# Gate projections of a hybrid block by seven half-size products, with sums of weights made by accumulating transfers

## Chip, core and metric

One NeuronCore of a Trainium2 chip runs the whole program. The metric is device time in microseconds (us), lower is better. TensorE (PE) multiplies, VectorE (DVE) and ScalarE (ACT) do the elementwise work, GpSimd (POOL) and SyncE (SP) issue transfers here. Each engine takes its instructions strictly in the order of its own queue.

## What is computed

One layer of a model with 512 tokens of 1024 channels, preceded by 16 learned tokens. In short, with `*` elementwise:

```python
h  = concat(meta, x)                       # 528 x 1024
xn = rms_norm(h, norm_mix_g)
u_rnn, u_gate, q, k, v, g_ret, ga, gb = split(xn @ w_in)
o_a = rg_lru(causal_dwconv(u_rnn)) * gelu(u_gate)
o   = retention(rotary(q), rotary(k) / 16, v)        # 4 heads, 256 / 512 wide
o_b = head_rms(o) * silu(g_ret)                      # 2048 columns of w_in
mixed = sigmoid(ga) * (o_a @ w_branch_rnn) + sigmoid(gb) * (o_b @ w_branch_ret)
h = h + mixed @ w_out
gate, val = split(causal_dwconv(rms_norm(h) @ w_up))
out = rms_norm(h + (gelu(gate) * val) @ w_down)[16:]
```

All of it is float32 at the interface. The gate projections of the title are `g_ret`, `ga` and `gb`: 4096 columns of `w_in`.

## The kernel before

Every matrix is used as two float16 parts, a high and a low one (`split`, lines 86 to 88: ACT makes the high part, DVE the low part). A product is then three float16 products, high by high, high by low and low by high (`project`, line 264). Activations lie with channels on partitions, two halves of 257 tokens beside each other, so one projection of 128 columns over 1024 channels is 8 x 3 x 2 = 48 matmuls of 257 columns.

Weights come in units of 1 MB or less. `unit_load` has SP load a unit into one of two raw buffers (`raw`, pool `wraw`) and returns two steps, each of which splits half of it; the fp16 result lies in a `wt` tile. A raw buffer is loaded anew when its last split has read it. `get(u)` forces a unit's steps out, `tick()` emits one more step if it is not too far ahead of the products (`ahead`). A gate unit has 8 x 128 channels and 256 columns, that is two projections.

Up to the gate branch of the recurrence the order of PE, ACT and DVE is written by hand; from `order.close()` on, a scheduler orders the instructions of each engine by its own estimates when the program is built. That order then stands in the queues.

After the rotation come, for four heads, `scores(h)` (line 578), `values(h)` (line 623), `retention_out(h)` (line 645) and `gated(h)`. `retention_out` makes four blocks of 24 products; DVE (L649) and ACT (L651) empty each block's accumulation tile. `gated` projects `g_ret` for four blocks of 128 columns, normalizes the head (L660 to L664), multiplies (L676, L680) and splits the result. PSUM is cut into four accumulation tiles of two banks. The mix then runs eight rounds: two gate projections with a sigmoid each (L713), ten and sixteen channel blocks of the two branches (results taken at L719 and L726), their sum and its split.

SBUF has a pool `big` of 11 large slots, one for each whole tensor of a stage.

Of the kernel before, what the change touches and what calls it, by code (L numbers as in the profile page):

```python
# [50 lines left out]
def hybrid_block_kernel(ctx, tc, x, meta, norm_mix_g, w_in, conv_w, conv_b, rg_a_w, rg_a_b,  # L51
# [11 lines left out]
    def psum_layout(**pools):  # L63
        """Cuts the eight banks anew; each tile waits only for the users of its own banks."""
# [15 lines left out]
    def bigt(shape, dtype, name):  # L80
        return big.tile(shape, dtype, name=name, tag="big")
# [10 lines left out]
    def load(dst, src):  # L92
        """Large loads, kept in this order on their queue."""
        if last_load[0] is None:
            last_load[0] = nc.sync.dma_start(dst, src)
        else:
            with tc.issue_after(last_load[0].ins):
                last_load[0] = nc.sync.dma_start(dst, src)

# [6 lines left out]
    def unit(nk, ncol, parts):  # L106
        units.append((nk, ncol, parts))
        return len(units) - 1
# [18 lines left out]
    def add_gr(h):  # L127
        u_gr[h] = [unit(8, 256, [(0, 0, kmaj(w_in, 0, 8, o_gr + 512 * h + 256 * a, 256))]) for a in range(2)]
# [10 lines left out]
    for c in range(KD):  # L139
        u_g.append(unit(8, 256, [(0, 0, kmaj(w_in, 0, 8, o_ga + P * c, P)),  # L140
                                 (0, P, kmaj(w_in, 0, 8, o_gb + P * c, P))]))
# [8 lines left out]
    wviews = []  # L150

    def unit_load(pieces=2):
        """Loads the next unit; returns the steps that split it into fp16 parts."""
        nk, ncol, parts = units[len(wviews)]
        raw = wraw.tile([P, 2048], F32, name="raw")
        wt = wsp.tile([P, 2, 2048], F16, name="wt")
# [4 lines left out]
        wviews.append([wt[:, a, :n].rearrange("p (k c) -> p k c", k=nk) for a in range(2)])  # L161
        hf = n // pieces

        def step(a):
            sl = slice(a * hf, (a + 1) * hf)
            return lambda: split(wt[:, 0, sl], wt[:, 1, sl], raw[:, sl], SW)

        return [step(a) for a in range(pieces)]
# [3 lines left out]
    ahead = [4]  # L172
    current = [0]

    def advance(upto):
        """Emits the split steps (two for each unit) up to this count, loads one unit further."""
        while done[0] < min(upto, 2 * len(units)):
            while len(wviews) < min(done[0] // 2 + 2, len(units)):
                steps.extend(unit_load())
            steps[done[0]]()  # L180
            done[0] += 1

    def get(u):
        current[0] = max(current[0], u)
        advance(2 * u + 2)
        return wviews[u]

    def tick(n=1):
        """Splits n more half units if that is not too far ahead of the products."""
        advance(min(done[0] + n, 2 * current[0] + 2 + ahead[0]))  # L190

# [13 lines left out]
    xh = bigt([P, KD, T + 3], F16, "xh")  # L205
    xl = bigt([P, KD, T + 3], F16, "xl")
# [3 lines left out]
    gmix = bigt([P, D], F32, "gmix")  # L210
# [11 lines left out]
    def norm_rows(src, rows, g_bc, xn):  # L222
        rs = rms_scale(src, rows, "n")
        for a in range(2):
            sl = slice(a * 512, (a + 1) * 512)
            nc.vector.scalar_tensor_tensor(xn[:rows, sl], src[:, sl], rs[:rows], g_bc[:rows, sl],
                                           op0=ALU.mult, op1=ALU.mult)

    def norm_transpose(rows, xhd, xld, s, xn):
        for a in range(2):  # L230
            pv = bank("ptr").rearrange("p (b c) -> p b c", c=P)
            for k in range(4):
                c0 = (4 * a + k) * P
                nc.tensor.transpose(pv[:, k, :rows], xn[:rows, c0:c0 + P], ident[:rows, :rows])
            sl = slice(4 * a, 4 * a + 4)
            split(xhd[:, sl], xld[:, sl], pv[:, :, :rows], s)

    def norm_tile(src, rows, g_bc, xhd, xld, s, xn):
        norm_rows(src, rows, g_bc, xn)
        norm_transpose(rows, xhd, xld, s, xn)  # L240
# [3 lines left out]
    for i in range(2):  # L244
        xt = bigt([P, 2, D], F32, f"xin{i}")
        xin.append(xt)
    xmeta = bigt([P, D], F32, "xmeta")
# [723 lines left out]
```

## Time and profile before

| | us |
|---|---|
| median of three timed runs | 1116.58 |
| their lowest and highest | 1115.74, 1117.15 |
| span of the profiled execution (first to last instruction; the page lists no other time of it) | 1115.0 |

The page shows one profiled execution on the core. Its head gives each engine's busy time; "PEclk" is the clock that PE was granted, in tenths of full speed, in 40 slices of the span. A row of groups reads: line, engine, operation, written tile <- read tiles, shape, count | busy us, mean ns of one | idle time of the engine just before, and what ended it. In the table of stages a row reads: from:to, length, then busy time and count for each engine, PE's clock, the busy share of the 16 DMA engines and GB/s. A row of transfers reads: written <- read, issuing queue, count, KB each, median us from issue to landing.

### The profile page before, as it was taken

What the parts mean: (1) busy time and instruction counts of PE and PEld (TensorE: products, weight loads), DVE (VectorE), ACT (ScalarE), POOL (GpSimd) and SP (SyncE); (2) the same over time, 40 slices, a digit from 0 to 9 for tenths busy, and PEclk for the clock granted to TensorE, in tenths of its full rate; (3) what the DMA queues carried; (4) which work ended last, traced back from release to release, by engine and by line L of the source; (5) the groups of instructions that cost most, each with busy time, mean ns of one, the idle gap of its engine ahead of it and who ended that gap; (6) DMA issues with size and microseconds to landing.
All of it is one profiled execution on the core that took longest, in us unless ns stands there. A gap on an engine that the chain in (4) does not pass through costs nothing.

```text
span 1115.0 us, 19885 instructions
## 1 busy us (share of the span) xinstructions
PE 1100.0 (99%) x8931; PEld 844.4 (76%) x8931; DVE 604.7 (54%) x827; ACT 453.1 (41%) x626; POOL 5.5 (0%) x15
## 2 busy tenths in 40 slices
PE   7999999999999999999999999999999999999997
PEld 5888888865767588888888886588888888854443
DVE  6875799965565466433333332485666656542203
ACT  6558954423434354322222221364444434422202
POOL 1000000000000000000000000000000000000000
PEclk9999999999999999999999999999999999999999
DMA  6432333532222222333334352053233232332101
GB/s 201 138 114 76 103 106 114 181 125 76 76 76 77 76 62 62 100 100 100 100 100 138 114 178 88 1 190 114 81 110 102 89 114 80 111 114 92 60 1 76
DMA packets 111242, 111.95 MB, mean 100 GB/s; under 512 B 2228, under 2 KB 100114, under 8 KB 111156
## 3 DMA queue, kind: packets, MB, share of 16 engines
q1 hardware_dynamic: 110868, 110.53, 31.2%
q8 instruction: 70, 1.15, 0.4%
q0 software_dynamic: 288, 0.14, 0.1%
q14 instruction: 16, 0.13, 0.0%
HBM read 108.56 MB, written 2.10 MB: 99 GB/s over the span
## 4 chain that ended last, share of the span: by engine, by line
PE 87%; DVE 6%; ACT 5%; DMA 1%; issue 0%; SPq 0%; DVEq 0%; ACTq 0%
PE ps L264 57%; PE pd L882 11%; PE ps L623 8%; PE ps L797 3%; PE ps L645 3%; PE ps L279 2%; DVE wt L88 2%; PE ps L578 1%; DVE xr L442 1%; ACT wt L87 1%; DMA raw<-in_w_in 1%; ACT L495 1%; ACT r L433 1%; ACT t L429 1%; DVE t L441 1%; DMA xmeta<-in_meta_tokens 0%
## 5 line engine op out<-in xcount | busy, mean ns | idle before, releaser
L264 PEld LDWEIGHTS <-wt 128*128 128x128 f16 x6528 | 634.5, 97 | 97.0 <-DVE t L534 1.4
L264 PE MATMUL ps<-xh,wt 128*128 128x257 f16 (+2 forms) x2080 | 321.6, 274 | 1.7 <-DVE t L534 1.7
L88 DVE SCALAR_TENSOR_TENSOR wt<-raw,wt 128x1024 f16<-128x1024 f32 (+2 forms) x200 | 228.5, 1165 | 150.5 <-ACT wt L87 149.6
L87 ACT ACTIVATE wt<-raw 128x1024 f16<-128x1024 f32 (+2 forms) x200 | 192.7, 1004 | 200.0 <-PE ps L264 82.5
L264 PE MATMUL ps<-x2h,wt 128*128 128x258 f16 x1440 | 218.8, 273 | 0.0
L264 PE MATMUL ps<-xl,wt 128*128 128x257 f16 (+2 forms) x1040 | 200.5, 274 | 0.0
L264 PE MATMUL ps<-x2l,wt 128*128 128x258 f16 x720 | 137.7, 272 | 0.0
L882 PE MATMUL pd<-wt,act 128*128 128x512 f16 x576 | 124.7, 379 | 0.0
L849 DVE SCALAR_TENSOR_TENSOR cv<-ps,vt,cv 128x512 f32<-128x512 f32 x96 | 72.0, 751 | 85.8 <-ACT cv L847 84.1
L882 PEld LDWEIGHTS <-act 128*128 128x128 f16 x576 | 56.3, 98 | 68.0 <-issue 0.5
L264 PE MATMUL ps<-ob,wt 128*128 128x257 f16 x768 | 87.1, 274 | 0.0
L623 PE MATMUL ps<-wt,xh 128*128 128x512 f16 x256 | 76.2, 379 | 0.0
L847 ACT ACTIVATE cv<-ps,vt,vt 128x512 f32<-128x512 f32 x48 | 37.3, 777 | 76.5 <-PE ps L264 74.2
L264 PE MATMUL ps<-oah,wt 128*128 128x257 f16 x320 | 50.0, 274 | 0.0
L623 PE MATMUL ps<-wt,xl 128*128 128x512 f16 x128 | 48.3, 379 | 0.0
L623 PEld LDWEIGHTS <-xh 128*128 128x128 f16 x256 | 24.8, 98 | 29.2 <-issue 1.4
L797 PE MATMUL ps<-wt,mx 128*128 128x512 f16 x192 | 44.5, 378 | 0.0
L726 DVE SCALAR_TENSOR_TENSOR sg<-ps,sg 128x514 f32<-128x514 f32 x8 | 5.5, 694 | 57.9 <-PE ps L264 57.9
L88 DVE SCALAR_TENSOR_TENSOR v<-ps,v 128x512 f16<-128x512 f32 x20 | 13.8, 690 | 39.4 <-ACT v L87 39.4
L87 ACT ACTIVATE act<-cv 128x512 f16<-128x512 f32 x24 | 15.1, 630 | 45.2 <-DVE cv L868 45.2
L713 ACT ACTIVATE sg<-ps 128x514 f32<-128x514 f32 x16 | 9.6, 599 | 56.9 <-PE ps L264 56.9
L279 PEld LDWEIGHTS <-wt 128*128 128x128 f16 x288 | 27.8, 97 | 6.1 <-DVE wt L88 1.0
(176 smaller groups left out, 832.5 us busy)
## 6 DMA issues: line engine op xcount, KB each, us to landing
raw<-in_w_in SPq DMA_DIRECT2D x33, 1024.0 KB, 5.1
raw<-in_w_up SPq DMA_DIRECT2D x24, 1024.0 KB, 5.2
raw<-in_w_down SPq DMA_DIRECT2D x12, 1024.0 KB, 4.9
raw<-in_w_in SPq DMA_DIRECT2D x18, 512.0 KB, 5.2
raw<-in_w_branch_ret SPq DMA_DIRECT2D x8, 1024.0 KB, 5.7
raw<-in_w_branch_rnn SPq DMA_DIRECT2D x8, 640.0 KB, 4.4
raw<-in_w_out SPq DMA_DIRECT2D x4, 1024.0 KB, 4.9
xin<-in_x SPq DMA_DIRECT2D x4, 512.0 KB, 8.8
```

Of the source, the lines that this page charges most:

```text
L87: nc.scalar.activation(hi, src, AF.Copy, scale=s)
L88: nc.vector.scalar_tensor_tensor(lo, src, s, hi, op0=ALU.mult, op1=ALU.subtract)
L264: nc.tensor.matmul(ps[:, hf, :n], w_[:, k, col:col + P], x_[:, k0 + k, c0:c0 + n], start=start and k == 0 and a == 0, stop=stop and k == n ...
L279: nc.tensor.matmul(ps[:, hf, :n], w_[:, k, col:col + P], x_[:, k, c0:c0 + n], start=k == 0 and a == 0, stop=k == KD - 1 and a == 2)
L429: nc.scalar.activation(part(half_t, n), part(half_r, n), AF.Tanh, scale=cpos[:, n:n + 1])
L433: nc.scalar.activation(r, r, AF.Exp, scale=cneg[:, n:n + 1])
L623: nc.tensor.matmul(pb, x_[:, k, XF + j0:XF + j0 + nb], w_[:, k % 4], start=i == 0, stop=i == 23)
L645: nc.tensor.matmul(ps[:, hf, s0 - lo_i:257], vt[:, va, b, d * P:(d + 1) * P], st[:, sa, o:o + hi_i - s0], start=i == 0, stop=i == len(todo ...
L797: nc.tensor.matmul(ps[:, n], mk[:, a, c0:c0 + P], w_[:, k % 2, n * 512:(n + 1) * 512], start=j == 0, stop=j == 23)
L847: nc.scalar.activation(vv_, ps[:, :, 2:258], AF.Identity, scale=vt2[:, 96 + ch:97 + ch], bias=b_ff[:, ch:ch + 1])
L849: nc.vector.scalar_tensor_tensor(vv_, ps[:, :, j:j + 256], vt2[:, 48 * j + ch:48 * j + ch + 1], vv_, op0=ALU.mult, op1=ALU.add)
L882: nc.tensor.matmul(pd[tt][n], a[:, va, k % 5, tt * P:(tt + 1) * P], w_[:, k % 2, n * 512:(n + 1) * 512], start=k == 0 and va == 0 and w_ i ...
```

## The change

**Seven products for eight.** For a gate unit the 1024 channels are taken in two halves of four blocks, the 256 columns in two halves of 128, and the tokens in their two halves. So the unit is a 2 x 2 product of blocks, which the kernel before makes of eight half products of 12 matmuls, and the changed one of seven, by a Strassen-like scheme (`fast_products`). The products use B11, B21 and B22 of the weights and four sums T1 to T4, and A11, A12 and A22 of the input and four sums F3, F5, F6, F7 (`make_forms`, made once).

**Sums of weights.** Most are made by transfers: POOL issues a transfer from HBM that adds the block 11 onto the block 12 in the raw buffer (L215) as soon as the buffer is loaded; after the lower rows are cut into fp16 (`cut_low`), another adds the upper rows onto the lower ones (L204; in the mix two transfers of half the size). DVE then adds the right columns of the lower rows onto the left ones of both halves in place (`sums`, L212), and the raw buffer is cut again. A gate unit is split into 3.5 tiles of 1024 columns where it was two.

**Running sums.** Of the seven products four accumulate in one bank, `pa`, and two in another, `pe`; ACT copies the running sum out (`keep`, L723) before the next product goes on in `pa`. DVE adds the parts (L740, L744, L751). The last two products of a unit are left pending and come later.

**PSUM and SBUF.** During the heads and the mix PSUM has two accumulation tiles and four single banks. The pool `big` becomes 43 pieces of about 2 KB per partition and four large slots, `wsp` ten half-size tiles.

```diff
-    big = ctx.enter_context(tc.tile_pool(name="big", bufs=11))
+    xp = ctx.enter_context(tc.tile_pool(name="xp", bufs=4))
+    pieces = ctx.enter_context(tc.tile_pool(name="pieces", bufs=43))
     wraw = ctx.enter_context(tc.tile_pool(name="wraw", bufs=2))
-    wsp = ctx.enter_context(tc.tile_pool(name="wsp", bufs=5))
+    wsp = ctx.enter_context(tc.tile_pool(name="wsp", bufs=10))
...
+    def fast_steps(rv, parts):
+        tiles = []
+        top, low = slice(0, 4), slice(4, 8)
+        left, right = slice(0, P), slice(P, 2 * P)
+        def cut(rows, cols):
+            def run():
+                t = wsp.tile([P, 2, 1024], F16, name="wt")
+                src = rv[:, rows, cols]
...
+                split(tv[0], tv[1], src, SW)
+            return run
+        def add_low():
+            for _, c0, ap in parts:
+                nc.gpsimd.dma_start(rv[:, low, c0:c0 + ap.shape[2]], ap[:, 0:4], accum_op=ALU.add)
+        def cut_low():
+            cut(low, slice(0, 2 * P))()
+            add_low()
+        def sums():
+            both = rv.rearrange("p (i k) c -> p i k c", i=2)
+            nc.vector.tensor_tensor(both[:, :, :, left], both[:, :, :, left],
+                                    both[:, 1:2, :, right].broadcast_to([P, 2, 4, P]), op=ALU.add)
+        nc.gpsimd.dma_start(rv[:, top, right], parts[0][2][:, 0:4, 0:P], accum_op=ALU.add)
...
+        return [cut_low, cut(top, left), sums,
+                cut(top, slice(0, 2 * P)), cut(low, slice(0, 2 * P))]
...
+    def make_forms(g):
...
+        for i in range(2):
+            for j in range(2):
+                v = t[i, j] = wtile("xt")[:, :TQ].rearrange("p (k c) -> p k c", k=2)
...
+                nc.vector.tensor_tensor(v, xh[:, k0:k0 + 2, c0:c0 + n], xl[:, k0:k0 + 2, c0:c0 + n], op=ALU.add)
+        a11, a12, a21, a22 = t[0, 0], t[0, 1], t[1, 0], t[1, 1]
+        nc.vector.tensor_tensor(a22, a22, a21, op=ALU.subtract)
+        nc.vector.tensor_tensor(a21, a11, a21, op=ALU.subtract)
+        nc.vector.tensor_tensor(a12, a11, a12, op=ALU.subtract)
+        nc.vector.tensor_tensor(a12, a12, a22, op=ALU.add)
+        nc.vector.scalar_tensor_tensor(a11, a22, -1.0, a11, op0=ALU.mult, op1=ALU.subtract)
+        for i, v in enumerate((a12, a22, a11, a21)):
+            xs = x_form_t[i // 2]
+            split(xs[:, 2 * (i % 2), ks], xs[:, 2 * (i % 2) + 1, ks], v, 1.0)
...
+    def fast_products(w, src, func, scale, finish):
...
+        def keep(dst, ps):
+            nc.scalar.activation(dst, ps[:, :257], AF.Copy)
...
+        pa = bank("pa")
+        product(pa, "B11", "A11", True)
+        keep(kept[:, h0], pa)
+        yield
+        pe = bank("pe")
+        product(pe, "T3", "F7", True)
+        yield
+        product(pa, "T2", "F6")
+        keep(kept[:, h1], pa)
+        yield
+        pb = bank("pb")
+        product(pb, "B21", "A12", True)
+        nc.vector.tensor_tensor(g0[:, h0], pb[:, :257], kept[:, h0], op=ALU.add)
+        yield
+        product(pa, "T1", "F5")
+        keep(last[:, h0], pa)
+        nc.vector.tensor_tensor(g1[:, h1], pe[:, :257], last[:, h0], op=ALU.add)
+        yield
+        product(pa, "B22", "F3")
+        nc.scalar.activation(g1[:, h0], pa[:, :257], func, scale=-scale)
+        nc.scalar.activation(g1[:, h1], g1[:, h1], func, scale=-scale)
+        finish(1, g1)
+        product(pe, "T4", "A22")
+        nc.vector.tensor_tensor(g0[:, h1], pe[:, :257], kept[:, h1], op=ALU.add)
+        nc.scalar.activation(g0[:, :TQ], g0[:, :TQ], func, scale=scale)
+        finish(0, g0)
...
     scores(0)
     values(0)
+    make_forms(0)
     scores(1)
     scores(2)
+    make_forms(1)
     values(1)
     scores(3)
+    psum_layout(acc=2, bank=4)
+    ahead[0] = 9
     retention_out(0)
...
     for c in range(KD):
...
+        run = fast_products(get(u_g[c]), x_forms, AF.Sigmoid, 1.0 / (SW * S_XN),
+                            lambda j, g: sg.update({j: g[:, :TQ].rearrange("p (a b) -> p a b", a=2)}))
+        next(run)
+        flush()
+        for _ in range(4):
+            next(run)
             tick()
+        pa = acc("pa")
+        project(pa, get(u_ba[c]), 0, oa_of, HH, NR)
+        for _ in run:
+            pass
```

Two places show how the queues change. Names carry buffer numbers; `raw` is a weight buffer, `wt` an fp16 weight tile, `ps` an accumulation tile. First, DVE around the first two blocks of `retention_out(2)`, before:

```order
L88 SCALAR_TENSOR_TENSOR v3_4140<-ps_4261,v3_4140 128x512
L88 SCALAR_TENSOR_TENSOR wt_4459<-raw_4458,wt_4459 128x1024 x2
L88 SCALAR_TENSOR_TENSOR v3_4140<-ps_4201,v3_4140 128x512
L88 SCALAR_TENSOR_TENSOR wt_4576<-raw_4575,wt_4576 128x1024
L649 TENSOR_SCALAR or2_4280<-ps_4282 128x514
L88 SCALAR_TENSOR_TENSOR wt_4576<-raw_4575,wt_4576 128x1024
L649 TENSOR_SCALAR or2_4280<-ps_4309 128x514
```

And DVE at the same place in the changed kernel:

```order
L92 SCALAR_TENSOR_TENSOR wt_4798<-raw_4670,wt_4798 128x1024
L92 SCALAR_TENSOR_TENSOR v3_4457<-ps_4428,v3_4457 128x512
L92 SCALAR_TENSOR_TENSOR v3_4488<-ps_4487,v3_4488 128x512
L92 SCALAR_TENSOR_TENSOR wt_4815<-raw_4670,wt_4815 128x512
L805 TENSOR_SCALAR or2_4507<-ps_4512 128x514
L212 TENSOR_TENSOR raw_4670<-raw_4670 128x8x128
L805 TENSOR_SCALAR or2_4508<-ps_4539 128x514
L92 SCALAR_TENSOR_TENSOR wt_4847<-raw_4670,wt_4847 128x1024
```

The first row is the low cut of the unit gr3a, after which POOL issues the transfer; the sums that need it (L212) now stand between the emptying of the block's first and second accumulation tile. Second, ACT where a round of the mix begins, before (two splits of 640 of a branch unit, the split of the round's result, two gate functions, splits again):

```order
L87 ACTIVATE wt_5457<-raw_5456 128x640 x2
L87 ACTIVATE mx0_4995<-sg_5046 128x514
L713 ACTIVATE sg_5333<-ps_5284 128x514
L713 ACTIVATE sg_5390<-ps_5341 128x514
L87 ACTIVATE wt_5565<-raw_5564 128x1024 x2
```

And the same place in the changed kernel:

```order
L91 ACTIVATE wt_5750<-raw_5634 128x1024
L91 ACTIVATE wt_5755<-raw_5634 128x512
L723 ACTIVATE kept_5568<-pa_5572 128x257
L91 ACTIVATE mx_5558<-g0_5237 128x514
L91 ACTIVATE wt_5861<-raw_5634 128x1024
L723 ACTIVATE kept_5568<-pa_5572 128x257
L723 ACTIVATE last_5569<-pa_5572 128x257
```

The split `wt_5861` reads the raw buffer after its sums, and the copy of the running sum of `pa` stands behind it; PE's product T1 goes on in `pa` after that copy.

More of the change, by code (lines that the diff above doesn't have):

```diff
@@ L160, in unit_load @@
             load(rv[:, k0:k0 + ap.shape[1], c0:c0 + ap.shape[2]], ap)
[L161 to L168, printed above, removed]
+        loaded.append(len(loaded))
+        if fast:
+            return fast_steps(rv, parts)
+        hk = nk // 2
```

444 lines of the change are left out of this document (250 added, 194 removed).

## Prediction

> **What bounds the kernel now.** I read the page's head first, then what TensorE (PE) waits for, then the chain that ended last, then busy time by stage.
>
> ```profile
> span 1115.0 us, 19885 instructions
> PE 1100.0 (99%) x8931; PEld 844.4 (76%) x8931; DVE 604.7 (54%) x827; ACT 453.1 (41%) x626; POOL 5.5 (0%) x15
> PEclk9999999999999999999999999999999999999999
> ```
>
> The reader sees one engine that is always busy, at its full clock. A busy PE need not be a PE that never waits, so the next view is its waits, in full (us in total, times, longest):
>
> ```profile
> PE ptr L234 <- DVE xn L226: 2.1, 2, 1.6
> PE ps L264 <- DVE t L534: 1.7, 2, 1.1
> PE ps L313 <- DVE warm L308: 1.4, 1, 1.4
> PE ptr L234 <- DVE xl L88: 1.3, 2, 1.1
> PE ps L279 <- DVE wt L88: 0.7, 1, 0.7
> PE ptr L234 <- DVE xo L226: 0.5, 1, 0.5
> PE ps L279 <- DVE xl L88: 0.4, 1, 0.4
> ```
>
> They add up to 8.1 us, and none is at a gate (L264 waits only for the rotation, L534). The chain that ended last gives the pitch of the products (start, us, what):
>
> ```profile
> 290.04 7.43 PE ps L645 x96
> ...
> 319.69 15.60 PE ps L623 x72
> ...
> 436.66 240.69 PE ps L264 x2160
> ```
>
> 240.69 us / 2160 = 111.4 ns for a product of 257 columns. So this kernel is as long as its list of products, and whatever takes products out shortens it by 111.4 ns each, as long as nobody makes PE wait. VectorE (DVE) and ScalarE (ACT) have room on average; the stages touched need their own rows:
>
> ```profile
> core 0: us, PE busy (x) PEld busy (x) DVE busy (x) ACT busy (x) POOL busy (x), PEclk, DMA share, GB/s
> 231.40:290.00 58.60, 58.58 (x370) 30.64 (x368) 34.20 (x72) 23.61 (x42) 0.00 (x0) 1.00 0.18 59
> 290.00:342.00 52.00, 52.00 (x412) 36.12 (x409) 28.44 (x42) 21.12 (x30) 0.00 (x0) 1.00 0.23 77
> 342.00:393.70 51.70, 51.70 (x408) 35.81 (x406) 28.13 (x34) 21.02 (x28) 0.00 (x0) 1.00 0.27 82
> 393.70:430.40 36.70, 36.70 (x387) 32.62 (x384) 25.70 (x33) 17.79 (x25) 0.00 (x0) 1.00 0.31 82
> 430.40:452.70 22.30, 22.30 (x200) 19.44 (x197) 13.71 (x16) 9.34 (x13) 0.00 (x0) 1.00 0.18 54
> 452.70:677.35 224.65, 224.65 (x2017) 196.43 (x2016) 71.47 (x79) 58.88 (x74) 0.00 (x0) 1.00 0.40 118
> ```
>
> 231 to 290 is scores and values, 290 to 452.7 the four heads' retention and gates, 452.7 to 677 the eight rounds of the mix. In the heads DVE works 28.44+28.13+25.70+13.71 = 96.0 us of 162.7, in the mix only 71 of 225.
>
> **What the change takes out.** 16 gate units lose one of eight half products each, 12 matmuls of 257 columns: 192 in all, and the two instruction lists differ by just that number of 128x257 products. 192 x 111.4 ns = **21.4 us**, half in the heads (10.7), half in the mix (10.7).
>
> **What it adds on DVE and ACT.** Prices of one, and their spacing when they follow one another:
>
> ```profile
> L88 DVE SCALAR_TENSOR_TENSOR wt<-raw,wt 128x1024 f16<-128x1024 f32 x176 | 210.4, 1218 | 149.8 <-ACT wt L87 149.6
> L87 ACT ACTIVATE wt<-raw 128x1024 f16<-128x1024 f32 x176 | 177.2, 1046 | 147.7 <-issue 46.5 <-PE pd L882 39.0 <-PE ps L264 30.1
> L649 DVE TENSOR_SCALAR or<-ps 128x514 f32<-128x514 f32 x16 | 10.9, 686 | 0.3
> L713 ACT ACTIVATE sg<-ps 128x514 f32<-128x514 f32 x16 | 9.6, 599 | 56.9 <-PE ps L264 56.9
> ```
>
> ```profile
> 446.09 1.22 DVE L88 SCALAR_TENSOR_TENSOR wt<-raw,wt 128x1024 f16<-128x1024 f32 x1
> 447.23 0.69 DVE L88 SCALAR_TENSOR_TENSOR ob<-g,ob 128x514 f16<-128x514 f32 x1
> 447.83 1.22 DVE L88 SCALAR_TENSOR_TENSOR wt<-raw,wt 128x1024 f16<-128x1024 f32 x1
> ```
>
> A 1024-column operation holds DVE for 447.23-446.09 = 1.14 us, a 514-column one for 0.60; by that slope one of 257 takes 0.33 (estimate). Each gate unit gains 1.5 tiles of splitting (1.14+0.60), the in-place sums of 1024 elements (1.14, priced as a split) and three additions of 257 (0.99): **3.9 us of DVE**, 31 in the heads, 31 in the mix. ACT gains 1.5 splits and three copies of 257 columns (0.38 each, from 599 ns for 514 and 1046 for 1024): 2.7 us. The input's seven forms add 26 DVE operations of 514 columns, 15.6 us, in the stage that had 34.2 of 58.6 busy: 49.8, still under PE's time; I put 1 us on it (0 to 4).
>
> **What it adds in waits.** For each gate unit, DVE cuts the lower weight rows, GpSimd (POOL) issues the accumulating transfer onto them, and the sums (L212) stand in DVE's in-order queue until it lands. Let L be the time from the cut's end to the landing of 512 KB. No accumulating transfer is in this trace; the nearest rows:
>
> ```profile
> raw<-in_w_in SPq DMA_DIRECT2D x33, 1024.0 KB, 5.1
> ...
> raw<-in_w_branch_ret SPq DMA_DIRECT2D x8, 1024.0 KB, 5.7
> ...
> out<-h SPq DMA_DIRECT2D x2, 256.0 KB, 2.0
> xmeta<-in_meta_tokens SPq DMA_DIRECT2D x1, 64.0 KB, 5.5
> v<-in_ffn_conv_w POOLq DMA_DIRECT2D x1, 64.0 KB, 6.8
> ...
> v<-in_norm_ffn_g POOLq DMA_DIRECT2D x1, 4.0 KB, 5.3
> ```
>
> Between 256 and 1024 KB a plain transfer grows by 3.1 us, so 512 KB would take 3.0: the lower end. The upper end is POOL's 6.8 for 64 KB plus twice 2.0 for moving 512 KB (it must also read what it adds to): 10.8. POOL's rows fall in the start's crowd, where even 64 KB on SP took 5.5 against 2.0 for 256 KB at the end, so I take **L = 6.0** (5.3 + 2.0, less a part of the crowd). The Trainium skill, DMA: Bandwidth & Descriptors, section "Anatomy of one DMA", fits a transfer issued from GpSimd with 2.0 us plus its bytes at 436 GB/s; by that 512 KB takes 3.2 us (estimate), and the holes below would all but vanish; the POOL rows of this trace, 5.3 and 6.8 for 4 and 64 KB, do not agree with it.
>
> *Heads.* Work that DVE has between a unit's low cut and its sums, by the order of the changed kernel at the spacings above: 2.8, 2.8, 0.6, 1.8, 2.4, 2.2, 3.6 us for the seven units whose sums fall here (gr1, gr2, gr3 and the first mix unit). With L = 6 the holes are 3.2+3.2+5.4+4.2+3.6+3.8+2.4 = 25.8 us. DVE then has 96.0+31.0+25.8 = 152.8 us to spend while PE has 162.7-10.7 = 152.0: level, before any wait of DVE for PE. A second row says where it hurts: evacuations of PSUM stand behind the sums, and the heads now have two accumulation tiles where there were four. One block of retention is 24 products, 7.43/4 = 1.86 us; emptying it takes 0.69 (DVE) and 0.60 (ACT), so a tile comes back in time only if DVE comes at once. Walking heads 2 and 3 with these numbers: the tile of the values before retention 2 comes back 1.1 us late (hole of gr2b); block 2's last tile waits 3.0 us because its predecessor's evacuation follows L212 of gr3a; block 3's last tile waits 3.8 us behind L212 of gr3b. Heads 0 and 1 have values (15.60/3 = 5.2 us for a bank) to hide in: 1 us. Together **9 us**, and some 5 us more for each microsecond more of L, since five of these holes pass on in full.
>
> *Copies of a running sum.* Three products of each unit go on accumulating in a bank that ACT must copy out first. The cover is 12 products, 12 x 111.4 = 1.34 us; needed are the end of the last product, the copy of 0.38 and two semaphores:
>
> ```profile
> L264 PE MATMUL ps<-xh,wt 128*128 128x257 f16 x1600 | 246.0, 273 | 1.1 <-DVE t L534 1.1
> ```
>
> A product ends 273-111 = 0.16 us after the next may start; with 0.1 assumed for two semaphores the need is 0.64. In each head B22 of the first unit follows its T1 after only 4 products (0.45 us): 0.3 late; and once per head a split, a table load or a gate function stands ahead of the copy: some 0.5. **3 us** for four heads.
>
> *Mix.* Per round PE now has 84+60+96 = 240 products, 26.7 us. From the start of T1 (time 0): the copy, the second split of the summed rows and its low part end at 4.2; the buffer is free, the next 1024-KB branch load (5.7) lands at 10; B22 and T4 end at 10.9; DVE and ACT do the branch cuts, the evacuation and the low cut until 15.9; the round's last product ends at 21.4, its evacuation and the next additions at 23.5. The sums may start there, the copy after them ends at 26.3, T1 is due at 26.7. So the two transfers of 256 KB have 23.5-15.9 = 7.6 us, and the second issue costs about 0.6:
>
> ```profile
> 1.44 0.68 POOL L348 DMA_DIRECT2D v<-in_rnn_conv_w  x1
> ...
> 5.20 0.51 POOL L356 DMA_DIRECT2D v<-in_ffn_conv_w  x1
> ```
>
> At L = 6 that is 6.6, in time: **0**, and 1:1 in seven rounds beyond L = 7.0.
>
> *At nothing:* SBUF in pieces adds seven transfers on SP and no compute that I could not count above; SP's cover is its own idle time:
>
> ```profile
> SPq L98 <- DVE wt L88: 936.9, 96, 42.7
> ```
>
> 12 MB more from HBM go beside a DMA share of 0.18 to 0.40. Without that cover the branch load of the mix walk would land later, at the same 1:1.
>
> **The sum.** -21.4 + 9 + 3 + 1 + 0 = **-8.4 us**: the profiled span of 1115.0 becomes 1106.6. The timed runs have a median of 1116.58, 1.6 above that span, so the time is **1108** us. Anything under 0.2% (2.2 us) is no change that a measurement of this kernel tells.
>
> **Rivals.**
> 1. *The transfers are prompt* (L of 3 to 4). For: 3.0 us by the plain rows, and the skill's fit, named above, is of this kind. Against: POOL's rows. The 9 us go, 1 to 4 remain: -17.4 to -20.4, some 1098. Chance 0.20.
> 2. *The transfers are slow, and the kernel gets slower.* The place is L212 in DVE's queue, in the heads and at each round's start. At L = 8.5 the heads cost 9+12.5 and the mix 7 x 1.5 = 10.5: -8.4+23 = +14.6, 1131. It decides from L = 7.3, where -8.4 + 6.5 + 2.1 is about nothing. For: 6.8 for a mere 64 KB, and an addition reads twice. Against: the start's crowd in that row. Chance 0.25.
> 3. *The copies cost more than the transfers.* If a split of 1.0 us has always just begun when a copy is due, the need is 1.64 against 1.34: 0.3 us at two places in 16 units, 9.6 in place of 3: -1.8, 1115, no change. Against: in the mix ACT is mostly idle at these places. Chance 0.10.
>
> That it doesn't do what it says can be left out, since the 192 products are gone from PE's list and PE is the bound.
>
> **How the numbers follow.** The forecast (1102 to 1114) has 0.45. Faster is forecast and rival 1, less the edge of the forecast's band: 0.64; no change rival 3 and that edge: 0.11; slower 0.25. The range goes from rival 1 at 1098 to L = 8.5, 1130.
>
> **What would show it.** Right: L264 and the new product line together have 192 products fewer, at 111 ns; DVE's idle time before L212 is put to a DMA, some 26 us in the heads; PE's waits appear at L801 and at the values, on DVE or ACT, 2 to 4 us each from retention 2 on, and hardly any in rounds 1 to 7. The POOL rows give L itself. Wrong: no PE waits at L801 (L was short), or a wait at T1 in every round of the mix (L over 7), or waits of the product line on ACT copies all through.

## The result, and the profile after

| | us |
|---|---|
| after, median of four runs | 1162.42 (1161.54 to 1165.17) |
| before, four runs on the same chip | 1116.16 (1115.35 to 1117.15) |
| ratio, with its 95% interval | 1.042 (1.0405 to 1.0435) |
| span of the profiled execution after, before | 1163.4, 1115.0 |

The change makes the kernel 4.2% slower; 1108 was forecast, with 1130 as the upper end. The profiled execution of the changed kernel is the slowest of its four (1165.17 us), so differences of stages below add up to a little more than the difference of the medians. One execution of e9, further below, fell into a second, slower state of the chip (1233.11 us, granted clock 0.855) and is left out of its time. First the head of the changed kernel's page, as it was read for before.

```profile
span 1163.4 us, 19961 instructions
...
PE 1098.4 (94%) x8739; PEld 832.7 (72%) x8739; DVE 689.3 (59%) x951; ACT 501.9 (43%) x730; POOL 57.2 (5%) x55
...
PEclk9899999989999998998999999999999999999999
```

PE has 192 instructions fewer (8931 before), so the change does what it says. But its busy time is the same as before, 1098.4 against 1100.0, and it now idles 65 us of the span where it idled 15. Work was removed and no busy time went: the clock row tells most of the reason. It shows slices at 8 where before had only 9s, so the products that are left ran slower there. The table of stages of the changed kernel (up to the scores, scores and values, heads, mix, rest; its columns as before) places both:

```profile
0.00:237.70 237.70, 223.48 (x1913) 186.86 (x1914) 188.42 (x282) 144.95 (x204) 6.95 (x16) 0.99 0.39 128
237.70:303.90 66.20, 61.67 (x371) 31.40 (x370) 50.32 (x100) 26.67 (x49) 3.86 (x3) 0.95 0.26 64
303.90:476.40 172.50, 154.19 (x1230) 111.71 (x1227) 116.17 (x152) 80.33 (x129) 19.27 (x15) 0.95 0.44 100
476.40:725.80 249.40, 228.58 (x1995) 196.61 (x1993) 117.09 (x146) 93.02 (x138) 27.16 (x21) 0.97 0.56 138
725.80:1163.00 437.20, 430.47 (x3242) 306.09 (x3241) 217.31 (x274) 156.97 (x213) 0.00 (x0) 1.00 0.26 88
```

And the same stages, cut at the same instructions, of the kernel before:

```profile
0.00:231.30 231.30, 223.65 (x1914) 187.35 (x1915) 186.63 (x279) 144.47 (x201) 5.47 (x15) 0.99 0.42 135
231.30:289.90 58.60, 58.58 (x371) 30.64 (x369) 34.10 (x72) 23.55 (x42) 0.00 (x0) 1.00 0.18 58
289.90:463.20 173.30, 173.30 (x1496) 133.26 (x1492) 98.86 (x126) 73.56 (x102) 0.00 (x0) 1.00 0.27 80
463.20:677.20 214.00, 214.00 (x1923) 187.17 (x1921) 68.68 (x75) 54.64 (x68) 0.00 (x0) 1.00 0.40 118
```

The start is 6.4 us longer, the scores 7.6, heads and mix together 421.9 - 387.3 = 34.6, the rest is the same (437.2 and 437.8): 48.6 in the first four. (A few products cross the border between heads and mix, so these two are taken together.) In heads and mix PE idles 18.3 + 20.8 = 39.1 us, where it idled 0. Its busy time there is 382.8; before's 387.3 less 192 x 111.4 ns is 365.9. Most of the 16.9 us between are products at a lower clock. The granted clock allows at most 0.05 x 172.5 + 0.03 x 249.4 = 16.1, and part of that fell into time in which PE stood anyway; e1 below, at full clock, still has 3.1 us of such busy time, which leaves 13.8 for the clock (an estimate). So 39.1 + 16.9 - 21.4 = 34.6: **the products are gone, and waits and longer busy time take two and a half times what they saved.** What PE waits for, in the changed kernel:

```profile
PE pa L718 <- ACT kept L723: 22.1, 10, 7.6
PE ps L801 <- ACT sq L807: 7.2, 2, 4.4
PE ps L778 <- DVE v L92: 6.2, 3, 4.7
...
PE ps L778 <- DVE sf L656: 4.2, 1, 4.2
```

The first row is, nearly all of it, T1 waiting for the copy of the running sum. Its name misleads: the copy takes 0.38 us, and it is late because it stands behind the split of the sums. The other rows are evacuations (`sq`, `v`, `sf`) that stand in a queue behind the sums, or behind the work that the sums held up. The transfers and the wait for them, from three views of the changed kernel (who DVE waits for; median us from issue to landing; POOL's groups):

```profile
DVE raw L212 <- DMA raw<-in_w_in: 59.9, 15, 8.0
```

```profile
raw<-in_w_in POOLq DMA_DIRECT2D x32, 256.0 KB, 4.9
...
raw<-in_w_in POOLq DMA_DIRECT2D x8, 512.0 KB, 6.0
```

```profile
L204 POOL DMA_DIRECT2D raw<-in_w_in x24 | 31.5, 1488 | 123.7 <-DVE wt L92 98.7 <-ACT g L748 25.0
L215 POOL DMA_DIRECT2D raw<-in_w_in x16 | 20.6, 1289 | 486.0 <-DVE t L606 222.1 <-DMA raw<-in_w_in 171.3 <-ACT sq L807 38.8
```

From its issue a transfer of 512 KB lands after 6.0 us, as forecast. But one issue holds POOL for about 1.28 us (L215; L204's mean mixes single issues and pairs), not 0.6, and POOL's queue is in order. A round of the mix, from one T1 (556.09) to the next, in the changed kernel (start, us, engine; idle time before and its end in brackets):

```profile
560.97 0.74 ACT L91 ACTIVATE wt<-raw 128x640 f16<-128x640 f32 x1 [1.71 <-PE pa L339]
564.32 0.74 ACT L91 ACTIVATE wt<-raw 128x640 f16<-128x640 f32 x1 [2.62 <-PE pa L339]
...
572.34 1.06 ACT L91 ACTIVATE wt<-raw 128x1024 f16<-128x1024 f32 x1 [3.10 <-PE pb L339]
573.43 1.23 DVE L92 SCALAR_TENSOR_TENSOR wt<-raw,wt 128x1024 f16<-128x1024 f32 x1 [3.12 <-ACT wt L91]
574.95 2.59 POOL L204 DMA_DIRECT2D raw<-in_w_in  x2 [1.93 <-DVE wt L92]
...
583.13 1.23 DVE L212 TENSOR_TENSOR raw<-raw 128x1024 f32<-128x1024 f32 x1 [3.47 <-DMA raw<-in_w_in]
...
585.35 0.37 ACT L723 ACTIVATE kept<-pa 128x257 f32<-128x257 f32 x1
```

The round takes 585.77 - 556.09 = 29.7 us; 26.7 was forecast. The low cut ends at 574.66, 18.6 us after T1, where I had 15.9: the splits of the branch unit and the cut itself wait for PE to finish with a weight tile (the brackets of the first three rows). Then the pair of transfers is issued in 2.59 us and has landed 8.5 us after the cut (583.13 - 574.66), where I had 6.6. That is the longest of the seven rounds, which have 7.2 to 8.5. The sums come too late by 3 us, and PE waits 2.80 for `kept`.

### The profile page after: what moved, and what is told of

The parts are those of the page before. It is cut to its first block, busy times and chain, and to the rows that moved or that the text cites. A ratio compares the mean times of both kernels' runs of the same rounds, so it can differ in the third digit from the quotient of the medians.

```text
span 1163.4 us, 19961 instructions
## 1 busy us (share of the span) xinstructions
PE 1098.4 (94%) x8739; PEld 832.7 (72%) x8739; DVE 689.3 (59%) x951; ACT 501.9 (43%) x730; POOL 57.2 (5%) x55
## 3 DMA queue, kind: packets, MB, share of 16 engines
q0 software_dynamic: 21408, 12.73, 8.4%
## 4 chain that ended last, share of the span: by engine, by line
PE 62%; DVE 16%; DMA 11%; ACT 8%; issue 2%; POOL 1%; SPq 0%; DVEq 0%; ACTq 0%; POOLq 0%
PE ps L339 27%; PE pd L1051 11%; DMA raw<-in_w_in 10%; DVE wt L92 6%; PE ps L778 5%; PE pa L339 4%; PE pa L718 4%; ACT wt L91 3%; PE ps L968 3%; PE pb L339 3%; PE ps L352 2%; PE pe L718 1%; DVE raw L212 1%; DMA raw<-in_w_up 1%; DVE t L607 1%
## 5 line engine op out<-in xcount | busy, mean ns | idle before, releaser
L339 PEld LDWEIGHTS <-wt 128*128 128x128 f16 x4992 | 487.2, 98 | 84.1 <-ACT wt L91 5.8
L92 DVE SCALAR_TENSOR_TENSOR wt<-raw,wt 128x1024 f16<-128x1024 f32 (+2 forms) x232 | 262.1, 1139 | 181.6 <-ACT wt L91 180.8
L91 ACT ACTIVATE wt<-raw 128x1024 f16<-128x1024 f32 (+2 forms) x232 | 225.1, 984 | 257.4 <-PE pd L1051 54.0
L339 PE MATMUL ps<-xh,wt 128*128 128x257 f16 (+2 forms) x1056 | 165.1, 276 | 7.7 <-ACT wt L91 5.5
L718 PEld LDWEIGHTS <-wt 128*128 128x128 f16 x1344 | 132.5, 99 | 47.7 <-issue 26.5
L1020 DVE SCALAR_TENSOR_TENSOR cv<-ps,vt,cv 128x512 f32<-128x512 f32 x96 | 72.1, 751 | 58.5 <-ACT cv L1018 56.8
L339 PE MATMUL ps<-xl,wt 128*128 128x257 f16 (+2 forms) x528 | 103.0, 277 | 0.0
L718 PE MATMUL pa<-xs,wt 128*128 128x257 f16 x576 | 76.2, 283 | 22.9 <-ACT kept L723 22.1
L339 PE MATMUL pb<-ob,wt 128*128 128x257 f16 x768 | 87.1, 274 | 0.0
L339 PE MATMUL pa<-oa,wt 128*128 128x257 f16 x480 | 57.2, 280 | 0.0
L212 DVE TENSOR_TENSOR raw<-raw 128x1024 f32<-128x1024 f32 x16 | 19.6, 1226 | 59.9 <-DMA raw<-in_w_in 59.9
L215 POOL DMA_DIRECT2D raw<-in_w_in x16 | 20.6, 1289 | 486.0 <-DVE t L606 222.1
L801 PE MATMUL ps<-sc,v 128*128 128x257 f16 (+4 forms) x384 | 34.3, 248 | 9.0 <-ACT sq L807 7.2
```

Source lines behind the costliest of these rows:

```text
L91: nc.scalar.activation(hi, src, AF.Copy, scale=s)
L92: nc.vector.scalar_tensor_tensor(lo, src, s, hi, op0=ALU.mult, op1=ALU.subtract)
L212: nc.vector.tensor_tensor(both[:, :, :, left], both[:, :, :, left], both[:, 1:2, :, right].broadcast_to([P, 2, 4, P]), op=ALU.add)
L339: nc.tensor.matmul(ps[:, hf, :n], w(aw, k, col, P), src(ax, k, c0, n), start=k == 0 and (aw, ax) == (0, 0), stop=k == nk - 1 and aw == 1)
L718: nc.tensor.matmul(ps[:, :257], w(wf, aw, k), src(xf_, ax, k), start=first and k == 0 and (aw, ax) == (0, 0), stop=k == 3 and aw == 1, ski ...
L801: nc.tensor.matmul(ps[:, hf, s0 - lo_i:257], vt[b][:, va, d * P:(d + 1) * P], st[SCP[b][0]][:, sa, o:o + hi_i - s0], start=i == 0, stop=i ...
```

## The experiments

Each is an edit of the changed kernel. A time without an interval is one run.

**e1, without the accumulating transfers:**

```diff
-            for _, c0, ap in parts:
-                nc.gpsimd.dma_start(rv[:, low, c0:c0 + ap.shape[2]], ap[:, 0:4], accum_op=ALU.add)
+            pass
...
-        nc.gpsimd.dma_start(rv[:, top, right], parts[0][2][:, 0:4, 0:P], accum_op=ALU.add)
```

> The changed kernel without its accumulating transfers (the sums of weights lack what they add; the seven products and everything else stay). Theory T, the waits for the transfers: DVE's 59.9 us at L212 and the PE waits in heads and mix that follow from them vanish, with the half clock behind them; PE waits in heads and mix fall from 39 us to under 10, time 1106 to 1122 us. Rival S, the structure (two accumulation tiles, copies of the running sum, slots of weight tiles): waits move to those, time stays over 1145.

Measured: **1110.46 us**, 52 below the changed kernel. Heads and mix, in its table of stages:

```profile
297.10:463.00 165.90, 161.67 (x1363) 120.73 (x1361) 127.54 (x170) 90.99 (x148) 0.00 (x0) 1.00 0.24 77
463.00:671.10 208.10, 207.31 (x1863) 181.06 (x1862) 105.36 (x128) 83.18 (x120) 0.00 (x0) 1.00 0.43 134
```

374.0 in place of before's 387.3, 13.3 saved of 21.4, at full clock. So copies, additional splits, additions and single banks together cost 8.1 us there (5.0 in which PE idles, 3.1 of busy time above 365.9), and the transfers all the rest.

**e2, the same sums made by DVE**, in place of the transfers:

```diff
-                nc.gpsimd.dma_start(rv[:, low, c0:c0 + ap.shape[2]], ap[:, 0:4], accum_op=ALU.add)
+            nc.vector.tensor_tensor(rv[:, low], rv[:, low], rv[:, top], op=ALU.add)
+            nc.vector.tensor_tensor(rv[:, top, right], rv[:, top, right], rv[:, top, left], op=ALU.add)
...
-        nc.gpsimd.dma_start(rv[:, top, right], parts[0][2][:, 0:4, 0:P], accum_op=ALU.add)
```

In the program the two additions stand right ahead of L212's, no longer right behind the low cut.

> The sums that transfers made are made by DVE in the raw buffer: one addition of 1024 and one of 512 columns more for a gate unit, 1.1 + 0.6 = 1.7 us, 28 us of DVE in all. T: nothing waits for a landing, DVE fits in the mix and nearly in the heads (96 + 31 + 14 = 141 of 152 us), time 1108 to 1125. S: over 1145.

Measured: **1115.95 us**, with heads and mix of 166.3 and 214.0 us. DVE, which the transfers were to spare, does 28 us more work and the kernel is 46 us faster.

**e3, the tick loads again.** The changed `tick` returns when no split is queued; it did not load the next unit then, as before's did.

```diff
             if done[0] == len(steps):
-                return
+                if len(loaded) == len(units):
+                    return
+                queue(unit_load())
```

> The changed kernel, but a tick that finds no split left loads the next unit, as the kernel before did. Theory: the wait of PE of 5.8 us at 42 us (L339 for ACT's wt) is a unit that is loaded only when it is needed; it goes, with the half clock behind it, and the time falls by 7 to 9 us to some 1154. Rival: the start is late for the pieces of SBUF, no change.

Measured: **1147.53 us**, 14.9 less, more than expected: the start falls by 8.3 us to 229.4, mix 249.4 to 244.1, heads and scores by 2 each (17.7 in all, against the slowest execution of the changed kernel). The cause at the start is in SP's queue. Before, then the changed kernel, then its PE:

```profile
30.99 14.92 SPq L98 DMA_DIRECT2D raw<-in_w_in  x3
```

```profile
41.05 0.37 SPq L102 DMA_DIRECT2D raw<-in_w_in  x1
...
48.05 0.62 PE L339 MATMUL ps<-xh,wt 128*128 128x267 f16 x2 [5.51 <-ACT wt L91]
```

Before, three loads stand in SP's queue from 31 us on and go as soon as a buffer is free. In the changed kernel the load comes at 41.05, when the unit is asked for, and PE stands 5.5 us.

**e4, eight products in the new layout** (gate units and projections as before, all else as changed; in the mix, for one):

```diff
-        run = fast_products(get(u_g[c]), x_forms, AF.Sigmoid, 1.0 / (SW * S_XN),
-                            lambda j, g: sg.update({j: g[:, :TQ].rearrange("p (a b) -> p a b", a=2)}))
...
+            project(ps, wg, m * P, xf, HQ, KD)
```

> The layout of the changed kernel (pieces, four large slots, half-size weight tiles, its tick) with the gate projections as before, eight half products and no sums. If the layout and the tick cost what the stages before the heads lost (6.4 + 7.5 us), 1127 to 1132 us. If the 7.5 us in the scores came from the gate units' loads and forms, 1121 to 1125. If the layout costs in the heads and the mix too, over 1135.

Measured: **1121.87 us**; its scores, heads and mix take 58.4, 173.2 and 214.0 to 214.1 us, the same as before, and its start 236.8. So SBUF in pieces costs nothing there, and the tick is all that is lost. With the loading tick as well, e8:

> Eight products as before the change, with the new layout of SBUF and PSUM and the tick that loads. If the tick is all that the layout version lost (e4: 1121.9, all of it at the start), the start goes from 236.8 to about 230 and the whole is 1114 to 1117, equal to before. Rival: loading early delays the decay table and the scores take 64 as in e3: 1119 to 1122.

Measured: **1114.33 us** beside 1115.48 for before, start 229.3. Confirmed.

**e5, sums by DVE and the loading tick** (the edits of e2 and e3). 

> All sums by DVE, and the tick that loads the next unit (the edits of e2 and e3 together). If the two losses are separate, their gains add: e2's 1115.9 less the 6 to 8 us that the first unit's late load costs at the start = 1108 to 1110, ratio about 0.993 of before; heads and mix as in e2 (166.3 and 214.0), start 229.4, scores 59.5 or with e3's late decay table up to 64. Rival: the loss at the start and the later ones are the same slack seen twice (loading early moves raw loads ahead of the decay table and into the rounds), so that scores take 64 and mix stays: 1113 to 1116, ratio 0.997 to 1.000.

Measured: **1108.21 us** against 1115.48, ratio 0.9936 (0.9923 to 0.9950). The late load at the start and the transfers' waits are separate losses: 7.7 us come off e2's time, and 7.5 off its start (236.8 to 229.3). What e3 gained beyond the start does not come a second time.

**e6, PE kept busy while it waits**, ahead of T1 in the mix (`fill` is 66 in the second round, 18 in the third to seventh):

```diff
+        for i in range(fill):
+            nc.tensor.matmul(pb[:, 257:512], w("B21", 0, 0), src("A12", 0, 0)[:, :255],
+                             start=i == 0, stop=i == fill - 1, skip_group_check=True)
...
```

> The changed kernel with 156 more 255-column products, which nobody reads, put on PE just ahead of T1 in the rounds 2 to 7 of the mix, where PE waits 1.9 to 7.9 us (66 in round 2, 18 each in rounds 3 to 7; 17 us of PE work at 111 ns). Theory C (the clock halves behind a wait and this is a cost of its own, 17.1 us at half speed in the mix = 8.5 us lost): with the waits filled the clock stays full, mix 241 to 243 in place of 249.4, the whole 1154 to 1156, although PE does 156 products more. Rival N (the half clock is not brought on by PE's idleness, or costs nothing since PE would wait for the transfers anyway): mix 249 or more, the whole 1162 or more.

Measured: **1156.97 us**, 5.4 less with 156 products more. Its mix:

```profile
474.90:717.60 242.70, 239.73 (x2150) 208.99 (x2149) 117.58 (x147) 92.86 (x138) 27.15 (x21) 1.00 0.57 142
```

The clock is 1.00 (0.97) and the stage 6.7 us shorter. The waits have not gone: 156 products (17.3 us) and 3.0 idle stand where 20.8 were idle. Only the slow products behind the waits went: without the 17.3, PE is busy for 222.4 us in place of 228.6. So the clock is a price of its own, 6.2 us in the mix; what it looks like in the changed kernel, around a wait of 7.65 us in the mix's second round, and around two others:

```profile
467.88 1.67 PE L718 MATMUL pa<-xs,wt 128*128 128x257 f16 x10 [2.10 <-ACT kept L723]
...
525.29 2.74 PE L718 MATMUL pa<-xs,wt 128*128 128x257 f16 x12 [7.65 <-ACT kept L723]
...
585.77 1.49 PE L718 MATMUL pa<-xs,wt 128*128 128x257 f16 x12 [2.80 <-ACT kept L723]
```

```profile
468.60:472.00 3.40, 3.40 (x14) 2.41 (x13) 1.79 (x3) 2.16 (x4) 0.00 (x0) 0.50 0.11 31
519.80:530.00 10.20, 4.71 (x23) 3.30 (x23) 4.39 (x6) 2.97 (x5) 0.00 (x0) 0.50 0.24 29
585.80:589.20 3.40, 3.40 (x31) 2.98 (x31) 2.21 (x4) 1.64 (x3) 0.00 (x0) 1.00 0.00 0
```

Twelve products take 2.74 us behind the long wait and 1.49 otherwise; the granted clock is 0.50 for 3.4 us behind a wait of 2.10, for 10.2 around one of 7.65, and 1.00 behind one of 2.80. The Trainium skill, TensorE: Matmul & The Clock Gate, section "Why this matters for your kernels", asks for no idle gap over about 3 us; its section "What's actually happening" has a window of about 3.4 us that runs freely. The steps of 3.4 agree. A wait of 2.10 us was enough once, and one of 2.80 not, so the limit of 3 us is no safe one here; whether it depends on where in a window a wait falls, no run here shows.

**e7, more weight tiles** (12 in place of 10), for which three small pieces go:

```diff
-    pieces = ctx.enter_context(tc.tile_pool(name="pieces", bufs=43))
+    pieces = ctx.enter_context(tc.tile_pool(name="pieces", bufs=40))
...
-    wsp = ctx.enter_context(tc.tile_pool(name="wsp", bufs=10))
+    wsp = ctx.enter_context(tc.tile_pool(name="wsp", bufs=12))
```

> The changed kernel with 12 fp16 weight tiles in place of 10 (and 40 small pieces in place of 43). Theory W (in the mix the low cut is late, 18.6 us after T1's start in place of 15.9, because the branch unit's splits wait for a free weight tile): the low cut comes up to 2.5 us sooner, PE's waits at T1 of the mix fall from 21 us to 5 to 10, half clock with them, mix 225 to 235, the whole 1138 to 1150. Rival R (the raw buffer or the transfer's own 8 us sets the round, and the weight tile wait only stands in line with it): mix 245 to 250, the whole 1158 to 1165.

Measured: **1143.44 us**, 19 less. Of PE's waits for `kept` one of 12.2 us stays, in the mix's second round; all others together are 2.5 us. From the second round's T1 on, the low cut now ends 12.1 to 12.6 us after T1, and no later round waits for `kept`. So the late low cut was the weight tiles' doing. But only half of the gain is in the mix, which stays above the expected 235: between the same products it is 12.3 us shorter, and the heads are 11.9 us shorter (161.2 in place of 173.1). The scores became longer, 69.0 us: the first unit's L212 now waits 7.12 us for its transfer amid the rotation, and PE 5.8 for the rotation.

**e11, the transfers without the addition**, in both places:

```diff
-                nc.gpsimd.dma_start(rv[:, low, c0:c0 + ap.shape[2]], ap[:, 0:4], accum_op=ALU.add)
+                nc.gpsimd.dma_start(rv[:, low, c0:c0 + ap.shape[2]], ap[:, 0:4])
```

> The changed kernel with the same transfers issued by POOL at the same places, but without the addition (they overwrite, so the sums T1 to T4 have other values; the amount of work is the same). Theory A (the addition itself makes them slow: reading and writing the target in SBUF): they land in 3 to 4 us in place of 4.9 (256 KB) and 6.0 (512 KB), an issue on POOL falls towards 0.6 us, holes before L212 fall from 60 to 25 us, the whole 1125 to 1145. Theory Q (a transfer issued by POOL costs this much whatever it does): landing and issue within 0.3 us of before, the whole 1158 to 1166.

Measured: **1125.99 us**, 36.4 less. Transfers of this kernel, and POOL's group of the issues behind the low cut:

```profile
raw<-in_w_in POOLq DMA_DIRECT2D x32, 256.0 KB, 3.5
...
raw<-in_w_in POOLq DMA_DIRECT2D x8, 512.0 KB, 4.1
```

```profile
L204 POOL DMA_DIRECT2D raw<-in_w_in x24 | 17.9, 748 | 116.0 <-DVE wt L92 81.4 <-DVE g L744 22.3 <-ACT v L91 11.8
```

DVE's wait before L212 falls from 59.9 to 21.8 us. The addition itself makes a transfer land 1.4 to 1.9 us later and the 24 issues of L204 take POOL 31.5 us with it and 17.9 without, 1.31 for 0.75 each. The queue rows of the two kernels, with addition and without (packets, MB), show another difference:

```profile
q0 software_dynamic: 21408, 12.73, 8.4%
```

```profile
q0 software_dynamic: 4000, 12.73, 3.6%
```

The same bytes go in five times as many packets; whether that is why the transfers are slower, no run separates. Up to two microseconds of landing and half a microsecond of issue per transfer decide over 36 of the kernel, since they fall on waits that had no slack left.

**e10, all mends but the transfers' removal**: the edits of e3 and e7, and the decay table loaded ahead of the rotation in place of behind it:

```diff
     dec = [piece([P, T + NM], F32, f"dec{h}") for h in range(HEADS)]
     for h in range(HEADS):
         nc.sync.dma_start(dec[h], decay_t[h])
```

> The changed kernel with its accumulating transfers, and all that cost beside them mended: the tick that loads, the decay table loaded ahead of the rotation, 12 weight tiles (40 pieces). If the four losses are separate, e7's 1143.4 loses the start's 8 and the scores' 10: 1124 to 1128; what is left over e5 (1108.2) then is the transfers' own price in DVE's queue, 16 to 20 us, in the heads (13 of waits) and at the mix's second round (12). Theory that the mends add up to a gain even with the transfers: below 1113. Rival that loading early crowds the raw buffers and brings waits back in the mix (e3's scores and heads kept theirs): 1130 to 1145.

Measured: **1141.26 us**, just 2.2 less than with the weight tiles alone. That is in the rival's range, but not in its place. The start is mended (230.7), the scores stay at 69.0, and the mix is as in e7 (238.0 and 238.7 us between the same products), its second round still waiting 11.7 us. The heads became 5.0 us longer, 166.2 in place of 161.2, with PE idle for 14.4 in place of 12.9 and a granted clock of 0.96 in place of 0.99; what causes that was not tested. And the decay table, which the chain of waits names ahead of the scores' gap, was not what made them late.

**Two tries at the best version**, both on sums by DVE and the loading tick. With e7's 12 weight tiles, e9: 

> e5 (sums by DVE, the tick that loads) with 12 weight tiles and 40 small pieces. e5 still loses 4.2 us at T1 of the mix's second round, where both raw buffers are loaded late, and 4 us of copies and evacuations in the heads. If the late loads there come from a wait for a weight tile, as the low cuts of e7 did, the 4.2 us and their half clock go: 1102 to 1105, ratio 0.988 to 0.991. Rival: that wait is set by the order of the two raw buffers, which more weight tiles do not change (e7 kept its one long wait at just this place): 1107 to 1110, ratio 0.993 as in e5.

Measured: **1112.87 us**, ratio 0.9971 (0.9960 to 0.9982): worse than without. The scores take 63.6 us, some 4 more than in e5. By the trace, with more tiles free the first gate unit's sums get into DVE's queue among the rotation's steps, all three of them, where e5 has only the first there; the next step of the rotation, L611 below, comes at 233.25, where e5 has it at 230.35. That PE's loss comes of this was not tested by a run:

```profile
229.07 0.70 DVE L610 TENSOR_TENSOR t<-ps,rope 128x528 f32<-128x528 f32 x1
229.69 1.22 DVE L211 TENSOR_TENSOR raw<-raw 128x1024 f32<-128x1024 f32 x1
...
233.25 0.70 DVE L611 TENSOR_TENSOR t<-ps,rope 128x528 f32<-128x528 f32 x1
```

With three raw buffers and 39 small pieces, e12:

```diff
-    pieces = ctx.enter_context(tc.tile_pool(name="pieces", bufs=43))
-    wraw = ctx.enter_context(tc.tile_pool(name="wraw", bufs=2))
+    pieces = ctx.enter_context(tc.tile_pool(name="pieces", bufs=39))
+    wraw = ctx.enter_context(tc.tile_pool(name="wraw", bufs=3))
```

> e5 (sums by DVE, the tick that loads) with three raw buffers in place of two and 39 small pieces in place of 43. e5 and e9 both wait 4 us at T1 of the mix's second round, and e9 shows that weight tiles do not set it. If two raw buffers set it (the round's gate unit is loaded only when the branch unit's splits have read their buffer), a third one takes the 4 us and the half clock behind it away: mix 208 to 210 in place of 213.8, the whole 1102 to 1105, ratio 0.988 to 0.991. Rival: the four pieces less make the rotation and the scores wait, as e9's 40 pieces did (63.5 us of scores in place of 59.4): 1107 to 1112, ratio 0.992 to 0.997.

Measured: **1104.64 us** against 1115.73, ratio 0.9899 (0.9882 to 0.9915), the fastest of all. Its mix:

```profile
458.10:666.20 208.10, 207.31 (x1863) 181.04 (x1861) 117.02 (x140) 82.29 (x118) 0.00 (x0) 1.00 0.43 135
```

208.1 us, at full clock and with 0.8 of idle time, where two buffers took 213.8: the wait in the second round was the raw buffers' doing. Fewer pieces cost nothing (scores 59.5), so what I had put on the pieces as a rival was not so.

## Why the prediction was wrong

The predicted sum was -8.4 us on the span, the measured one +48.4. The 56.8 us between them, by its own terms:

1. **-21.4 for 192 products: right.** The count is exact, and with the transfers away heads and mix run at full clock and come out 13.3 shorter.
2. **L = 6.0 and holes of 25.8 us in the heads: right in size.** From issue to landing the trace has 6.0 us, and DVE waits 28.0 us at the seven L212 there (the sum; single holes differ, see 3). The size of L was in part luck: it was taken from small plain transfers in the start's crowd, while e11 has a plain 512 KB at 4.1 us, and the addition makes up the rest.
3. **Heads at 9 + 3: too low.** PE idles 18.3 us. Three waits were as walked: the values' tile behind gr2b (forecast 1.1, measured 1.21, at a hole of 4.57 for 4.2), block 2's last tile (3.0, 2.76) and block 3's (3.8, 4.44). The unit before them, gr2a, is the step that failed here. The walk gave it a hole of 5.4 us and no wait of PE that it names; the hole was 8.02 us, and PE waited 4.68 for a tile of the values before retention 2 (`v` below, which stands behind L212). DVE had no work between cut and sums, and this transfer landed 8.0 us after its issue, with that of L215 issued 1.8 ahead of it. The term for copies was low too: e1 leaves 8.1 in heads and mix, with the evacuations of two tiles in it, where 3 was put. The changed kernel there:

```profile
382.13 1.28 POOL L215 DMA_DIRECT2D raw<-in_w_in  x1 [16.33 <-ACT last L723]
383.91 1.28 POOL L204 DMA_DIRECT2D raw<-in_w_in  x1 [0.49 <-DVE wt L92]
```

```profile
391.99 1.23 DVE L212 TENSOR_TENSOR raw<-raw 128x1024 f32<-128x1024 f32 x1 [8.02 <-DMA raw<-in_w_in]
393.13 0.68 DVE L92 SCALAR_TENSOR_TENSOR v<-ps,v 128x512 f16<-128x512 f32 x1
393.87 1.01 PE L778 MATMUL ps<-wt,xh 128*128 128x512 f16 x2 [4.68 <-DVE v L92]
```

4. **Mix at 0: the step that failed most.** "At L = 6 that is 6.6, in time" rested on a low cut that ends 15.9 us after T1 and a second issue of 0.6. The cut ended 18.6 to 20.9 us after T1, and once, ahead of the second round's T1, 24.7, since I walked DVE and ACT without asking whether a weight tile was free, and the pair took 7.2 to 8.5. PE idles 20.8 us in the mix, 19.8 of them in waits for `kept`. e7 shows the first half of this (the cut at 12.1 to 12.6, no such wait from the third round on), e11 the second. In the second round e7's twelve tiles did not help; with sums by DVE the raw buffers were what it waited for (e12).
5. **A wait was priced at its own length.** The clock halves behind it, and no term held that: some 13.8 us in heads and mix, which is the 16.9 less the 3.1 that e1 keeps at full clock. e6 shows 6.2 of it in the mix; in the heads no run takes the clock apart from the waits.
6. **Forms at 1: the forms were not the point.** The holes were counted for "the seven units whose sums fall here", in the heads. The first gate unit's sums fall into the scores, where they cost 7.6 us; e1, with the forms and without the transfers, has 58.8 us there, 0.2 more than before. In the changed kernel, DVE and POOL there:

```profile
236.34 1.23 DVE L92 SCALAR_TENSOR_TENSOR wt<-raw,wt 128x1024 f16<-128x1024 f32 x1 [1.73 <-ACT wt L91]
...
239.82 1.28 POOL L215 DMA_DIRECT2D raw<-in_w_in  x1 [8.40 <-DMA dec<-decay]
240.59 1.81 POOL L204 DMA_DIRECT2D raw<-in_w_in  x1
...
249.04 1.23 DVE L212 TENSOR_TENSOR raw<-raw 128x1024 f32<-128x1024 f32 x1 [5.79 <-DMA raw<-in_w_in]
250.19 1.23 DVE L656 SCALAR_TENSOR_TENSOR sf<-ps,dec 128x257 f32<-128x257 f32 x3
```

   The cut ends at 237.6, its transfer is issued at 240.6, because L215 of the next unit stands ahead of it in POOL's queue and waits for a load; the scores' evacuation (L656) stands behind L212.

7. **"At nothing" for loads and layout: right for the pieces (e4), wrong for the loads.** SP's idle time was no cover, since the changed `tick` did not use it: 6.4 us at the start, and e3 gains 14.9 by it in all. I had read that function for its limit, not for its return.

In numbers: idle time of heads and mix 39.1 in place of 12, 27.1 more; busy time beyond the products' own 16.9 (clock 13.8, the rest e1's 3.1); scores 7.6 in place of 1, 6.6 more; start 6.4. Together 57.0.

Of the rivals, the second had the place and the mechanism (L212 in DVE's queue, in the heads and at each round's start), and its deciding point, 7.3 us from the cut's end, was passed in five of the seven rounds of the mix (up to 8.5) and at one unit of the heads (8.0). Its price, 1131, lacked the clock, the scores and the start. The third named the wrong mechanism: T1's waits carry the name of the copy, but without the transfers PE waits 0.4 us for `kept` in all; its size, 9.6, was not far from the 8.1 that the new structure costs without transfers. The first, prompt transfers, would not have been enough by itself: e11's plain ones are that, and the kernel is still at 1126.0.

The Trainium skill, DMA: Bandwidth & Descriptors, section "Anatomy of one DMA", gives 3.2 us for 512 KB by its fit (an estimate). These runs have 4.1 without the addition and 6.0 with it. By the fit the forecast would have been lower yet.

Three things stay open. What part of e3's gain in the mix comes from loads and what from a clock that halved at other waits was not separated. Accumulating transfers with a third raw buffer were not tried, so what made their second round of the mix wait was not tested. And the two costs of the addition, later landing and longer issue, were taken away only together.

## What to carry to other kernels

Price a new wait on the engine that bounds the kernel at its length and the slower clock behind it, and walk the whole loop for it: buffers and weight tiles that must be free, what stands ahead in the issuing engine's queue, what stands behind the waiting instruction. Here an engine that was 41% idle on average was a cheaper place for an addition than a transfer that must land between two of its instructions. And look at what the bounding engine still waits for once the first cause is gone: sums by another engine, earlier loads and a third raw buffer, one after the other, turned 4.2% of loss into 1.0% of gain.

## What was not expected of the hardware

- An accumulating transfer of 512 KB took 6.0 us and its issue 1.28 us of POOL; the same one without the addition took 4.1 and 0.75, and the queue's packets fell from 21408 to 4000.
- PE's granted clock was 0.50 for 3.4 us behind a wait of 2.10 us and for 10.2 around one of 7.65, and 156 products that nobody reads, put into such waits, made the kernel 5.4 us faster.
